# A hybrid decoder layer on one core: the order of the first transfers and the way through the last norm

## The chip, the cores and the metric

One Trainium2 chip, one of its cores. The metric is the time of one execution on the device in microseconds (us), the median of several runs; lower is better. One more execution was taken with the hardware profiler, and its trace is what the tables and rows below come from. The engines are TensorE (PE, and PEld for its weight loads), VectorE (DVE), ScalarE (ACT), GpSimd (POOL) and SyncE (SP), which issues the DMA transfers.

## The reference

One layer for 272 prompt tokens (16 learned ones and 256) and 8 decoding tokens together, 280 columns, with D_MODEL 2048 and D_FF 5504, all in float32. Cut to what matters here:

```python
def layer_norm(x, g, b):
    mu = jnp.mean(xf, axis=-1, keepdims=True)
    var = jnp.mean(jnp.square(xf - mu), axis=-1, keepdims=True)
    return ((xf - mu) * lax.rsqrt(var + LN_EPS)).astype(x.dtype) * g + b

def swiglu(x, w_gate, w_up, w_down):
    return (jax.nn.silu(x @ w_gate) * (x @ w_up)) @ w_down

def decoder_layer(x, ...):
    x = layer_norm(ALPHA * x + 0.5 * swiglu(x, f1_g, f1_u, f1_d), ln1_g, ln1_b)
    m, s_ret, s_hg = token_mixer(x, pos, s_ret, s_hg, prompt, w_in, lb, hg_norm_g, w_out)
    x = layer_norm(ALPHA * x + m, ln2_g, ln2_b)
    x = layer_norm(ALPHA * x + 0.5 * swiglu(x, f2_g, f2_u, f2_d), ln3_g, ln3_b)
    return x, s_ret, s_hg
```

The mixer projects to 10 times the width, runs two recurrent branches (retention with 8 heads, HGRN2 with 16), merges them by gates and projects back. The 16 learned tokens are dropped from the output, so behind the mixer there are 264 columns.

## The kernel before

Activations lie with features on the partitions and tokens along the free dimension: a tensor of width 2048 is 16 chunks (`KC`) of 128 features by 280 (or 264) columns. Weights are packed by the host into blocks of 128x128 in exactly the order in which they are used; eight blocks are a unit of 512 KB. `stream` hands them out: at the first block of a unit it issues the DMA into a tile `raw` (SyncE, L143), ScalarE rounds it to the short format `whi` (L145), VectorE takes the rest, `wlo` (L147). Each of the three tiles has three buffers, so unit u+3 waits for unit u. Activations are split in the same way into `xh` and `xl` (`split`, L176 and L177). `dense` then makes each product of two float32 blocks from three matmuls in the short format: high by high (L169), high weights by low activations (L170), low weights by high activations (L171), accumulated in PSUM.

The order of instructions on TensorE is that of the program. On the other engines a scheduler orders them by priority when the program is built, and `high_priority` puts the loading of a unit ahead of what stands earlier in the program. At the start this gives SyncE the order: three units, two chunks of tokens, three units, and so on; one DMA brings one chunk of tokens (L365).

`ffn` runs groups of two gate and two up blocks (four PSUM banks), 16 steps of k each; a group reads four blocks for each token chunk, so a unit covers two chunks. Then 16 down products, one chunk each, with 43 steps of k. `Norm` takes up each finished chunk: `chunk` adds alpha times the low and the high part of x to the product (L242, L243), `shifted` subtracts a common shift (the mean over chunk 0, found by `shift`), squares it on ScalarE and adds both to two running sums on VectorE. For the first two norms (`lead`) the chunk also goes on, scaled, to the next projection, whose matmuls begin before the statistics are known; `first` corrects their results, and `normalise` makes the normed chunks meanwhile. For the third norm `stats` sums over partitions by two products with a matrix of ones in full float32 (L285, L286; TensorE makes two matmul instructions of each such product), takes mean and variance, and `rsqrt` the reciprocal root with one Newton step, after a load of ScalarE's table for that function. Then `normalise` centres each chunk (VectorE), scales it by gain and root (VectorE, L320), adds the bias (ScalarE, L327) and stores it (SyncE, L328), 16 stores.

The scheduler also orders VectorE's and ScalarE's work in the mixer, where threads of small matmuls run between the dense ones.

Of the kernel before, what the change touches and what calls it, by code (L numbers as in the profile page):

```python
# [10 lines left out]
F32 = mybir.dt.float32  # L11
# [7 lines left out]
P = 128  # L19
# [12 lines left out]
U = 8  # L32


WP = P + 4
XP = 296
KSC = 1.0 / 16.0
LEVELS = (1, 2, 4, 8, 16, 32, 64)
MASKED = 5
# [58 lines left out]
def trunk(ctx: ExitStack, tc: tile.TileContext, A, O):  # L98
# [34 lines left out]
    nc.vector.memset(eps_h, EPS)  # L133


    def stream(w_dram):
        n_units = w_dram.shape[0]
        state = {"u": -1, "j": U, "hi": None, "lo": None}

        def load(u):  # L140
            with tc.high_priority():
                raw = wp.tile([P, U, P], F32, tag="raw", name=f"raw{u}", bufs=3)
                nc.sync.dma_start(raw, w_dram[u].rearrange("p (b c) -> p b c", b=U))  # L143
                hi = wp.tile([P, U, WP], F32R, tag="whi", name=f"whi{u}")[:, :, :P]
                nc.scalar.copy(hi, raw)  # L145
                lo = wp.tile([P, U, WP], F32R, tag="wlo", name=f"wlo{u}")[:, :, :P]
                nc.vector.tensor_tensor(out=lo, in0=raw, in1=hi.bitcast(F32), op=ALU.subtract)  # L147
# [12 lines left out]
        return block  # L160

    def dense(block, nk, outs, xhi, xlo, cols=slice(0, T), hook=None):
# [51 lines left out]
    def row_tile(name, n=T):  # L214
        return rp.tile([P, n], F32, tag=name, name=name)

    class Norm:
# [14 lines left out]
        def row(self, name):  # L232
            return row_tile(name)[:, : self.n]

        def chunk(self, m, f):
            n = self.n
            a = ALPHA if self.whole else 2.0 * ALPHA
            dx = row_tile(f"d{m}", T + 1)
            self.dx[m] = dx
            self.d[m] = d = dx[:, :n]  # L240
            x0 = xh[m].shape[1] - n
            nc.vector.scalar_tensor_tensor(out=d, in0=xl[m][:, x0:].bitcast(F32), scalar=a, in1=f, op0=ALU.mult, op1=ALU.add)  # L242
            nc.vector.scalar_tensor_tensor(out=d, in0=xh[m][:, x0:].bitcast(F32), scalar=a, in1=d, op0=ALU.mult, op1=ALU.add)  # L243
            if self.lead:
                nc.gpsimd.memset(dx[:, n : n + 1], 1.0)
            if self.c is None:
                self.waiting.append(m)
            else:
                self.shifted(m)

        def shift(self):
            n = self.n
            pc = mx_bank("pc")
            nc.tensor.matmul(pc[:, :n], ones, self.d[0], start=True, stop=True)
            self.c = self.row("lnc")
            nc.scalar.mul(self.c, pc[:, :n], 1.0 / P)
            self.s1, self.s2 = self.row("ls1"), self.row("ls2")
            for m in self.waiting:
                self.shifted(m)

        def shifted(self, m):
            n, d = self.n, self.d[m]
            sub(d, d, self.c)
            if m == 0:
                nc.scalar.copy(self.s1, d)
                nc.scalar.activation(self.s2, d, AF.Square)
            else:
                q = self.row("lnq")
                nc.scalar.activation(q, d, AF.Square)
                add(self.s1, self.s1, d)  # L270
                add(self.s2, self.s2, q)
            if self.lead:
                x_tiles(m, f"g{self.which}", n + 2)
                g = self.g[:, m : m + 1]
                dx = self.dx[m][:, : n + 1]
# [36 lines left out]
                ys.append(y)  # L312
            return ys

        def normalise(self, out=None):
            for c in range(KC):
                d = self.d[c]
                g, b = self.g[:, c : c + 1], self.b[:, c : c + 1]
                sub(d, d, self.mean)
                nc.vector.scalar_tensor_tensor(out=d, in0=d, scalar=g, in1=self.r, op0=ALU.mult, op1=ALU.mult)  # L320
                if out is None:
                    x_tiles(c, self.which, self.n)
                    nc.scalar.activation(xh[c], d, AF.Identity, bias=b)  # L323
                    nc.vector.scalar_tensor_tensor(  # L324
                        out=xl[c], in0=d, scalar=b, in1=xh[c].bitcast(F32), op0=ALU.add, op1=ALU.subtract)
                else:
                    nc.scalar.activation(d, d, AF.Identity, bias=b)  # L327
                    nc.sync.dma_start(out[c], d)  # L328

    def ffn(i, w_up, w_dn, which, before=None):  # L330

        n = T if before is None else TL
        cols = slice(0, n)
        with tc.tile_pool(name=f"h{i}", bufs=1) as hp:
            hh, hl = [None] * FC, [None] * FC
            block = stream(w_up)
            for gn, grp in enumerate(ffn_up_groups()):
                bank = acc_bank if gn % 2 == 0 else mx_bank
                outs = [bank(f"up{gn}_{j}") for j in range(len(grp))]
# [5 lines left out]
                for j in range(ng):  # L345
# [16 lines left out]
    with tc.tile_pool(name="inp", bufs=2) as ip:  # L362
        for c in range(KC):
            x0 = ip.tile([P, T], F32, tag=f"x0{c}", name=f"x0{c}", bufs=1)
            nc.sync.dma_start(x0, A["x"][:, c, :])  # L365
            x_tiles(c, 0)
            split(xh[c], xl[c], x0)
# [13 lines left out]
    nc.sync.dma_start(dec, A["dec"])  # L381
    nc.sync.dma_start(sel, A["sel"])

    norm1 = ffn(1, A["w_up1"], A["w_dn1"], 1)


    with tc.tile_pool(name="yp", bufs=1) as yp:
# [408 lines left out]
        norm2 = Norm(2, TL, True, True)  # L796
        for gn, grp in enumerate(out_groups()):
            outs = [acc_bank(f"wo{m}") for m in grp]
            dense(block, KC, outs, yh, yl, slice(0, TL), (lambda k: k == 6 and norm2.shift()) if gn == 1 else None)
            for m, o in zip(grp, outs):  # L800
                norm2.chunk(m, o[:, :TL])


    norm3 = ffn(2, A["w_up2"], A["w_dn2"], 3, norm2)
    norm3.stats()
    norm3.normalise(O["y"])


# [110 lines left out]
```

## Time and profile before

| | |
|---|---|
| median of 3 runs | 2869.44 us |
| the runs | 2877.39, 2869.44, 2869.11 us |
| the profiled execution | 2873.62 us |
| its span, first to last instruction | 2871.8 us |
| granted TensorE clock, mean | 0.994 |
| busy TensorE, VectorE, ScalarE | 2823.0, 1700.5, 1326.4 us |
| read from memory | 502.12 MB, 186 GB/s with what is written |

Busy time counts an engine's instructions, and a matmul's duration reaches over the beginning of the next, so a busy TensorE says only that matmuls follow each other. In rows of a timeline the first number is the start in us from the span's start, the second the time from the first to the last of the merged instructions; "xh<-x" names output and input tile, "x3" the count, and the bracket gives how long the engine was idle before and what ended that. Rows with "DMA" or "issue" ahead of a line come from the chain that ended last, followed back from the last instruction.

### The profile page before, as it was taken

The numbers are of one execution on the slowest core, as the hardware profiler recorded it, in microseconds if no ns is written. First come the engines' busy times: TensorE is split into PE (matmuls) and PEld (weight loads), VectorE is DVE, ScalarE is ACT, GpSimd is POOL, SyncE is SP. The second block draws the span as 40 slices with busy tenths as digits, with TensorE's granted clock in tenths as the row PEclk, the third lists the DMA queues.
The fourth block names the chain that finished last, engine by engine and source line by source line (L and its number), as shares of the span: only waits on it lengthen the run. The fifth ranks groups of instructions, "written<-read, shape, count | busy, mean of one in ns | idle before, by whom it ended". The sixth has DMA issues, their size and how long they took to land.

```text
span 2871.8 us, 54200 instructions
## 1 busy us (share of the span) xinstructions
PE 2823.0 (98%) x22642; PEld 2769.2 (96%) x22642; DVE 1700.5 (59%) x2690; ACT 1326.4 (46%) x1929; POOL 3.4 (0%) x38
## 2 busy tenths in 40 slices
PE   8999999999999999999999999999999999999997
PEld 8999999999999999899989898999999999999997
DVE  5444444455586766676757575766894444445555
ACT  4443334433353564545455554545454444444333
POOL 0000000000000000000000000000000000000000
PEclk9999999999999999999999999999999999999998
DMA  6555555555556665656665657564555555555553
GB/s 212 170 171 173 169 170 170 170 173 169 169 184 213 200 228 190 215 191 222 193 216 195 220 179 229 168 226 164 177 180 180 183 184 180 181 183 178 183 179 131
DMA packets 155717, 536.25 MB, mean 187 GB/s; under 512 B 18064, under 2 KB 27856, under 8 KB 155472
## 3 DMA queue, kind: packets, MB, share of 16 engines
q1 hardware_dynamic: 155472, 532.80, 57.5%
q8 instruction: 177, 2.90, 0.4%
q14 instruction: 68, 0.56, 0.1%
HBM read 502.12 MB, written 30.61 MB: 186 GB/s over the span
## 4 chain that ended last, share of the span: by engine, by line
PE 95%; ACT 1%; DMA 1%; DVE 1%; issue 0%; SPq 0%; ACTq 0%; DVEq 0%
PE up L170 12%; PE up L171 12%; PE up L169 12%; PE dn L169 6%; PE dn L170 6%; PE dn L171 6%; PE pj_g_r L169 1%; PE pj_v_r L169 1%; PE pj_k_r L169 1%; PE pj_f L169 1%; PE pj_g_h L169 1%; PE pj_v_r L170 1%; PE pj_k_r L170 1%; PE pj_f L170 1%; PE pj_f L171 1%; PE pj_k_r L171 1%
## 5 line engine op out<-in xcount | busy, mean ns | idle before, releaser
L147 DVE TENSOR_TENSOR wlo<-raw,whi 128x1024 fp32r<-128x1024 f32 x868 | 1062.7, 1224 | 916.6 <-ACT whi L145 911.5
L145 ACT CAST whi<-raw 128x1024 fp32r<-128x1024 f32 x868 | 909.4, 1048 | 1169.1 <-PE up L170 484.7
L169 PE MATMUL up<-xh,whi 128*128 128x280 f32 (+1 forms) x2688 | 772.9, 288 | 9.0 <-ACT xh L176 9.0
L170 PE MATMUL up<-xl,whi 128*128 128x280 f32 (+1 forms) x2688 | 774.3, 288 | 1.1 <-DVE xl L177 1.0
L171 PE MATMUL up<-xh,wlo 128*128 128x280 f32 (+1 forms) x2688 | 773.4, 288 | 0.0
L169 PEld LDWEIGHTS up<-xh,whi 128*128 128x128 f32 x2688 | 506.5, 188 | 9.2 <-ACT xh L176 9.2
L170 PEld LDWEIGHTS up<-xl,whi 128*128 128x128 f32 x2688 | 506.2, 188 | 1.8 <-DVE xl L177 1.8
L171 PEld LDWEIGHTS up<-xh,wlo 128*128 128x128 f32 x2688 | 506.6, 188 | 0.0
L169 PE MATMUL dn<-hh,whi 128*128 128x280 f32 (+1 forms) x1376 | 397.1, 289 | 0.0
L170 PE MATMUL dn<-hl,whi 128*128 128x280 f32 (+1 forms) x1376 | 395.8, 288 | 0.0
L171 PE MATMUL dn<-hh,wlo 128*128 128x280 f32 (+1 forms) x1376 | 395.8, 288 | 0.0
L170 PEld LDWEIGHTS dn<-hl,whi 128*128 128x128 f32 x1376 | 259.0, 188 | 0.1
L169 PEld LDWEIGHTS dn<-hh,whi 128*128 128x128 f32 x1376 | 258.9, 188 | 0.1
L171 PEld LDWEIGHTS dn<-hh,wlo 128*128 128x128 f32 x1376 | 258.6, 188 | 0.0
L169 PE MATMUL pj_g_r<-xh,whi 128*128 128x264 f32 x256 | 82.9, 324 | 0.0
L169 PE MATMUL pj_g_h<-xh,whi 128*128 128x264 f32 x256 | 77.3, 302 | 0.0
L170 PE MATMUL pj_i_h<-xl,whi 128*128 128x280 f32 x256 | 74.9, 293 | 2.4 <-DVE xl L324 2.4
L169 PE MATMUL pj_i_h<-xh,whi 128*128 128x280 f32 x256 | 75.0, 293 | 1.3 <-ACT xh L323 0.7
L169 PE MATMUL pj_v_r<-xh,whi 128*128 128x280 f32 x256 | 76.0, 297 | 0.0
L169 PE MATMUL pj_k_r<-xh,whi 128*128 128x280 f32 x256 | 75.9, 297 | 0.0
L170 PE MATMUL pj_v_r<-xl,whi 128*128 128x280 f32 x256 | 74.7, 292 | 0.0
L170 PE MATMUL pj_k_r<-xl,whi 128*128 128x280 f32 x256 | 74.6, 291 | 0.0
(310 smaller groups left out, 5154.2 us busy)
## 6 DMA issues: line engine op xcount, KB each, us to landing
raw<-in_w_up SPq DMA_DIRECT2D x344, 512.0 KB, 3.5
raw<-in_w_in SPq DMA_DIRECT2D x320, 512.0 KB, 3.5
raw<-in_w_dn SPq DMA_DIRECT2D x172, 512.0 KB, 3.5
smr<-in_sr SPq DMA_DIRECT2D x32, 512.0 KB, 5.6
out_srs<-smr SPq DMA_DIRECT2D x32, 512.0 KB, 4.3
raw<-in_w_out SPq DMA_DIRECT2D x32, 512.0 KB, 3.5
smh<-in_sg SPq DMA_DIRECT2D x16, 512.0 KB, 4.3
out_sgs<-smh SPq DMA_DIRECT2D x16, 512.0 KB, 6.1
```

The source lines that it names most:

```text
L145: nc.scalar.copy(hi, raw)
L147: nc.vector.tensor_tensor(out=lo, in0=raw, in1=hi.bitcast(F32), op=ALU.subtract)
L169: nc.tensor.matmul(o, wh, h, start=k == 0, stop=False)
L170: nc.tensor.matmul(o, wh, l, start=False, stop=False)
L171: nc.tensor.matmul(o, wl, h, start=False, stop=k == nk - 1)
```

## The change

At the start, the first unit is loaded in two parts of two and six blocks, the tokens in larger pieces, and the first transfers get fixed turns (0 first): chunk 0 on ScalarE's DMA queue, the unit's first part, its second, chunk 1, chunks 2 and 3, chunks 4 and 5. The other tokens (6 to 7, 8 to 11, 12 to 15) stand in the program's order. Seven products of the ones matrix with itself run on TensorE ahead of the first dense matmul; their results aren't used.

In the norms, the residual of a chunk (`residual`) is computed ahead of its dense product as soon as the shift is known (`ahead`), with the shift subtracted in it; behind the product one addition is left.

In the last norm `finish` takes the place of `stats` and `normalise`: the two sums over partitions take the running sums up to chunk 14, and chunk 15 and its square as second products of their own; the root is computed with the bias inside ScalarE's function, whose table an early activation loads behind the last gate block; five chunks are centred by VectorE, eleven by TensorE (identity by chunk plus identity by minus mean, in PSUM); VectorE multiplies by the root, ScalarE applies gain and bias, and two chunks go out in one store.

```diff
+WARM = 7
+PE_CENTRED = 11
...
+    def turn(n):
+        return tc.high_priority(offset=tc.tile_snap_priority() + 100 * (9 - n))
...
-        def load(u):
-            with tc.high_priority():
-                raw = wp.tile([P, U, P], F32, tag="raw", name=f"raw{u}", bufs=3)
...
+        def load(u, parts=((0, U, tc.high_priority),)):
...
+            for j0, j1, when in parts:
+                with when():
+                    nc.sync.dma_start(raw[:, j0:j1, :], src[:, j0:j1, :])
+                    nc.scalar.copy(hi[:, j0:j1, :], raw[:, j0:j1, :])
+                    nc.vector.tensor_tensor(out=lo[:, j0:j1, :], in0=raw[:, j0:j1, :], in1=hi[:, j0:j1, :].bitcast(F32), op=ALU.subtract)
...
+        if at_once:
+            state["hi"], state["lo"] = load(0, ((0, 2, lambda: turn(1)), (2, U, lambda: turn(2))))
+            state["u"] = state["j"] = 0
...
-        def chunk(self, m, f):
+        def residual(self, m, other, op):
...
-            nc.vector.scalar_tensor_tensor(out=d, in0=xl[m][:, x0:].bitcast(F32), scalar=a, in1=f, op0=ALU.mult, op1=ALU.add)
+            nc.vector.scalar_tensor_tensor(out=d, in0=xl[m][:, x0:].bitcast(F32), scalar=a, in1=other, op0=ALU.mult, op1=op)
             nc.vector.scalar_tensor_tensor(out=d, in0=xh[m][:, x0:].bitcast(F32), scalar=a, in1=d, op0=ALU.mult, op1=ALU.add)
...
+        def chunk(self, m, f):
+            if self.d[m] is not None:
+                add(self.d[m], self.d[m], f)
+                self.shifted(m)
+                return
+            self.residual(m, f, ALU.add)
...
+        def ahead(self, m):
+            if self.c is not None:
+                self.residual(m, self.c, ALU.subtract)
...
-                q = self.row("lnq")
+                self.q = q = self.row("lnq")
                 nc.scalar.activation(q, d, AF.Square)
+                if m == KC - 1 and not self.lead:
+                    return
...
+        def finish(self, out):
+            n = self.n
+            p1, p2 = mx_bank("p1"), mx_bank("p2")
+            for p, s in ((p1, self.s1), (p2, self.s2)):
+                nc.tensor.matmul(p[:, :n], ones, s, start=True, stop=False)
+            for p, s in ((p1, self.d[KC - 1]), (p2, self.q)):
+                nc.tensor.matmul(p[:, :n], ones, s, start=False, stop=True)
+            neg, v, r, t = self.row("lnc"), self.row("rv"), self.row("rr"), self.row("rt")
+            nc.scalar.activation(t, p1[:, :n], AF.Square, scale=1.0 / D)
+            nc.vector.scalar_tensor_tensor(out=v, in0=p2[:, :n], scalar=1.0 / D, in1=t, op0=ALU.mult, op1=ALU.subtract)
+            nc.scalar.mul(neg, p1[:, :n], -1.0 / D)
+            nc.scalar.activation(r, v, AF.Abs_reciprocal_sqrt, bias=eps_l)
...
+            centred = list(self.d)
+            for c in range(KC):
+                if c < KC - PE_CENTRED:
+                    add(self.d[c], self.d[c], neg)
                 else:
-                    nc.scalar.activation(d, d, AF.Identity, bias=b)
-                    nc.sync.dma_start(out[c], d)
+                    pd = (acc_bank if c % 2 else mx_bank)("pd")[:, :n]
+                    centred[c] = pd
+                    nc.tensor.matmul(pd, ident, self.d[c], start=True, stop=False)
+                    nc.tensor.matmul(pd, ident, neg, start=False, stop=True)
+            yo = ctx.enter_context(tc.tile_pool(name="yo", bufs=1))
+            for c0 in range(0, KC, 2):
+                y = yo.tile([P, 2, n], F32, tag=f"y{c0}", name=f"y{c0}")
+                for c in (c0, c0 + 1):
+                    mul(self.d[c], centred[c], r)
+                    nc.scalar.activation(
+                        y[:, c - c0, :], self.d[c], AF.Identity, scale=self.g[:, c : c + 1], bias=self.b[:, c : c + 1])
+                nc.sync.dma_start(out[c0 : c0 + 2].rearrange("c p t -> p c t"), y)
...
+            if before is not None:
+                warm = hp.tile([P, 1], F32, tag="warm", name="warm")
+                nc.scalar.activation(warm, sg[:, 0:1], AF.Abs_reciprocal_sqrt, scale=0.0, bias=eps_l)
             block = stream(w_dn)
             norm = Norm(which, n, False, i == 1)
             for m in range(KC):
                 o = acc_bank(f"dn{m}")
+                norm.ahead(m)
                 dense(block, FC, [o], hh, hl, cols, (lambda k: k == 6 and norm.shift()) if m == 1 else None)
                 norm.chunk(m, o[:, :n])
...
+        pw = mx_bank("pw")
+        for _ in range(WARM):
+            nc.tensor.matmul(pw[:, :P], ones, ones, start=True, stop=True)
+        up1 = stream(A["w_up1"], at_once=True)
+        for n, queue, c0, c1 in ((0, nc.scalar, 0, 1), (3, nc.sync, 1, 2), (4, nc.sync, 2, 4), (5, nc.sync, 4, 6)):
+            with turn(n):
+                tokens(queue, c0, c1)
+        for c0, c1 in ((6, 8), (8, 12), (12, KC)):
+            tokens(nc.sync, c0, c1)
...
-    norm3.stats()
-    norm3.normalise(O["y"])
+    norm3.finish(O["y"])
```

The norm behind the mixer calls `ahead` in the same way, and `tokens` issues one DMA for its chunks and splits each.

More of the change, by code (lines that the diff above doesn't have):

```diff
@@ L133, in trunk, with stream @@
     nc.vector.memset(eps_h, EPS)
[L136 removed]
+    def turn(n):
+        return tc.high_priority(offset=tc.tile_snap_priority() + 100 * (9 - n))
+    def stream(w_dram, at_once=False):
         n_units = w_dram.shape[0]
         state = {"u": -1, "j": U, "hi": None, "lo": None}
[L140 to L147 removed]
+        def load(u, parts=((0, U, tc.high_priority),)):
+            raw = wp.tile([P, U, P], F32, tag="raw", name=f"raw{u}", bufs=3)
+            hi = wp.tile([P, U, WP], F32R, tag="whi", name=f"whi{u}")[:, :, :P]
+            lo = wp.tile([P, U, WP], F32R, tag="wlo", name=f"wlo{u}")[:, :, :P]
+            src = w_dram[u].rearrange("p (b c) -> p b c", b=U)
+            for j0, j1, when in parts:
[3 more added lines that the diff above has]
+                    nc.vector.tensor_tensor(out=lo[:, j0:j1, :], in0=raw[:, j0:j1, :], in1=hi[:, j0:j1, :].bitcast(F32), op=ALU.subtract)
             return hi, lo
@@ L332, in ffn @@
+    def ffn(i, block, w_dn, which, before=None):
         n = T if before is None else TL
@@ L362, in trunk, with tokens @@
     with tc.tile_pool(name="inp", bufs=2) as ip:
[L363 to L367, printed above, removed]
+        def tokens(queue, c0, c1):
+            x0 = ip.tile([P, c1 - c0, T], F32, tag=f"x0{c0}", name=f"x0{c0}", bufs=1)
+            queue.dma_start(x0, A["x"][:, c0:c1, :])
+            for c in range(c0, c1):
+                x_tiles(c, 0)
+                split(xh[c], xl[c], x0[:, c - c0, :])
+        pw = mx_bank("pw")
[7 more added lines that the diff above has]
+            tokens(nc.sync, c0, c1)
         mf = ip.tile([P, MASKED + 1, 2 * P], F32, tag="mf", name="mf", bufs=1)
```

27 lines of the change are left out of this document (14 added, 13 removed).

## The prediction

> **What bounds the kernel now.** I read the page first, then the start and the end as timelines, then the chain of waits and some windows in between. The page:
>
> ```profile
> span 2871.8 us, 54200 instructions
> PE 95%; ACT 1%; DMA 1%; DVE 1%; issue 0%; SPq 0%; ACTq 0%; DVEq 0%
> ```
>
> The second line is the chain that ended last: 95% of the span is TensorE. Where TensorE streams, nothing that the change does to another engine can shorten the time; it can pay only where TensorE stands, and that is mostly ahead of the first matmuls and behind the last. Of the start, the timeline of SyncE's DMA issues, of ScalarE, of VectorE and of TensorE, and one row of the chain (start us, us, what, idle before in brackets):
>
> ```profile
> 0.73 1.33 SPq L143 DMA_DIRECT2D raw<-in_w_up  x3
> 2.11 1.06 SPq L365 DMA_DIRECT2D x<-in_x  x2
> 6.83 2.87 SPq L143 DMA_DIRECT2D raw<-in_w_up  x3
> 9.75 5.62 SPq L365 DMA_DIRECT2D x<-in_x  x10
> ...
> 4.50 1.04 ACT L145 CAST whi<-raw 128x1024 fp32r<-128x1024 f32 x1 [2.18 <-DMA raw<-in_w_up]
> 7.04 1.05 ACT L145 CAST whi<-raw 128x1024 fp32r<-128x1024 f32 x1 [0.25 <-DMA raw<-in_w_up]
> 8.00 0.74 ACT L176 CAST xh<-x 128x280 fp32r<-128x280 f32 x2
> 19.11 1.05 ACT L145 CAST whi<-raw 128x1024 fp32r<-128x1024 f32 x1 [0.65 <-PE up L170]
> 28.43 1.05 ACT L145 CAST whi<-raw 128x1024 fp32r<-128x1024 f32 x1 [2.05 <-PE up L170]
> ...
> 5.58 3.77 DVE L147 TENSOR_TENSOR wlo<-raw,whi 128x1024 fp32r<-128x1024 f32 x3 [4.57 <-ACT whi L145]
> ...
> 8.47 0.60 PE L169 MATMUL up<-xh,whi 128*128 128x280 f32 x1 [8.47 <-ACT xh L176]
> 12.50 0.43 PE L169 MATMUL up<-xh,whi 128*128 128x280 f32 x1
> 12.73 0.43 PE L170 MATMUL up<-xl,whi 128*128 128x280 f32 x1
> 13.26 0.29 PE L170 MATMUL up<-xl,whi 128*128 128x280 f32 x1
> 13.39 0.29 PE L171 MATMUL up<-xh,wlo 128*128 128x280 f32 x1
> ...
> 12.13 3.75 DMA x<-in_x
> ```
>
> Three units of weights (512 KB each) come ahead of the first tokens, so the first matmul waits until 8.47. Then three more weight issues, which wait for free buffers (6.83 to 9.70), stand in SyncE's queue ahead of token chunk 2, and the chain waits for it until 15.88. Up to 12.96 the matmuls follow each other in 0.23 us, afterwards in 0.13: half rate, then full. What all that costs: the cast at 19.11 waits for the matmuls of unit 1 and the one at 28.43 for those of unit 4, so 72 matmuls take 9.32 us, 0.129 each; 47 of them are done by 19.1, so a stream without a gap would have begun at 13.0.
>
> The end, as timelines of VectorE, TensorE, ScalarE and SyncE, and the DMA issues:
>
> ```profile
> 2851.51 0.43 DVE L242 SCALAR_TENSOR_TENSOR d<-xl,dn 128x264 f32<-128x264 f32 x1 [6.55 <-PE dn L171]
> 2853.39 0.71 PE L285 MATMUL p<-ls,ones 128*128 128x264 f32 x2 [1.92 <-DVE ls L188]
> 2853.94 0.68 PE L286 MATMUL p<-ls,ones 128*128 128x264 f32 x2
> 2854.14 0.39 ACT L288 ACTIVATE lnc<-p 128x264 f32<-128x264 f32 x1 [0.75 <-PE p L285]
> 2855.26 0.43 DVE L291 SCALAR_TENSOR_TENSOR lnq<-p,lnq 128x264 f32<-128x264 f32 x1
> 2856.26 1.28 ACT L199 ACT_TABLE_LOAD   x1
> 2857.55 0.42 ACT L199 ACTIVATE rr<-rv 128x264 f32<-128x264 f32 x1
> 2859.72 0.42 DVE L202 SCALAR_TENSOR_TENSOR rr<-rt,rr 128x264 f32<-128x264 f32 x1
> 2860.41 4.93 DVE L320 SCALAR_TENSOR_TENSOR d<-d,lnp,rr 128x264 f32<-128x264 f32 x12
> 2861.47 7.84 SPq L328 DMA_DIRECT2D out_y<-d  x16
> 2867.97 0.92 ACT L327 ACTIVATE d<-d,lnp 128x264 f32<-128x264 f32 x2 [0.57 <-DVE d L320]
> ...
> out_y<-d SPq DMA_DIRECT2D x16, 132.0 KB, 1.8
> ```
>
> The last dense product is read at 2851.51 and the span ends at 2871.8: 20.3 us in which TensorE does two products with the ones matrix. The reciprocal root is ready at 2860.14, VectorE scales 16 chunks at 0.41 each, and 2.9 us after ScalarE's last pass (2868.89) the last store has landed and the program has closed.
>
> **The start.** The change puts token chunk 0 first on ScalarE's DMA queue, and on SyncE's: two blocks of unit 0, its other six, chunk 1, chunks 2 and 3, chunks 4 and 5, and only then unit 1. Units 0 to 2 land 1.27 us apart (4.50 to 7.04 for two), 403 KB per us. Unit 0 landed at 4.50, so the first 268 KB (two blocks and chunk 0) by 3.9; 652 KB, all of unit 0, at 4.85; chunks 1 to 5 by 6.6 (1352 KB); unit 1 by 7.85 (1864 KB). Two casts of about 0.4 (chunk 0 is half of 0.74; a quarter of a unit lies between that and a quarter of 1.04) put the first matmul at 4.75 where it was 8.47. Its six matmuls and the other 18 of unit 0 wait for six blocks' cast and subtraction (three quarters of 1.04 and of 1.26, the mean of the three subtractions), so from 6.7 on they stream, and end near 8.8. Unit 1 is cast from 7.85 to 8.9 and subtracted by 10.15; its third matmul, the first that reads the low part, waits for that. The 21 matmuls that are then left of the 47 take 2.7, and unit 1's buffer is free at 13.1 where it was 19.1: 6.0 us. At the tokens' pace of the trace (ten of 140 KB in 5.62 us, 249 KB per us, waits included) 840 KB of tokens take 1.3 us longer, and 4.7 are left. With pairs in one transfer the 0.56 that one issue took there matters less, so I stay near the upper end: **5.6** (4.7 to 6.0).
>
> Seven products of the ones matrix run ahead of the first matmul. The trace has such products of 264 and 280 columns; 128 columns at 0.47 per 280 (rows below) are 0.21, and at half rate 0.43: 1.5 to 3.0 us from about 1.1, over by 4.1, and the loads are not there before 4.3, so they cost nothing. Half rate lasted from 8.47 to 12.96, 4.5 us from the first matmul; counted from the first ones product it ends near 5.6. If it doesn't, 24 matmuls of unit 0 at 0.23 last from 4.75 to 10.3, still about the time at which unit 1's low part is there: 0 to 0.5. ScalarE issues chunk 0's transfer (about 0.43 of its queue) when it has nothing else until 3.9. Under "DMA: Bandwidth & Descriptors", section "Anatomy of one DMA", the Trainium skill counts about 2.0 us fixed for each DMA beside bytes at 436 GB/s, and its rules ask for large transfers, which speaks against cutting unit 0 in two; the trace has three transfers landing 1.27 us apart, so the fixed part overlaps when issues follow each other. By that page alone the first 128 KB would be there 2.3 us after the issue at 0.73, at 3.0, and the sum would still hang on unit 1's subtraction.
>
> **The middle.** The residuals of a chunk are computed ahead of its dense product (two VectorE passes), with the shift subtracted in the first; afterwards one addition is left. Passes before: three; after: three. At the first two norms TensorE goes on with the next projection and reads chunk 15 last, so the shorter step there hides behind matmuls, as before: 0. The early activation `warm` moves a table load of 1.28 to the start of the second down projection, where ScalarE idles around 2 us between casts: 0, and it waits only for the last gate tile.
>
> **The end.** Before: two residual passes, the shift, a sum, then TensorE at 2853.39. After: one addition (2851.51 to 2851.95). The products of ones with the two running sums are queued right behind the last dense matmul, and those with chunk 15 and its square follow them. The price of one ones product of full precision:
>
> ```profile
> 817.32 0.64 PE L285 MATMUL p<-ls,ones 128*128 128x280 f32 x2
> 817.79 0.63 PE L286 MATMUL p<-ls,ones 128*128 128x280 f32 x2
> ```
>
> 0.47 to the next one at 280 columns, 0.443 at 264; in the end of the trace 0.55 (2853.39 to 2853.94). Four from 2851.47 end at 2853.25; the mean's are streamed by 2852.8 and readable 0.25 later (0.71 from start to end of such a product, 0.44 to 0.47 of it stream). ScalarE squares the mean and negates it (0.39 each, as `lnc`): minus mean at 2853.85. VectorE's variance, ScalarE's root without table load at 2854.45, three VectorE passes (2.2 before, from 2857.97 to 2860.14): root at 2856.65. From then 16 multiplications at 0.41 end at 2863.2, if their operands are there. Eleven chunks are centred by TensorE, two identity products each; the first of the 22 needs no mean, 21 wait for minus mean and nothing else is queued behind them: 21 times 0.443 is 9.3, from 2853.85 to 2863.15, readable at 2863.4. So TensorE sets the end, not VectorE: multiplication 0.43, ScalarE 0.5, at 2864.4. Then the 2.9 of before, and for the pair, 132 KB more at the stores' pace (16 in 7.84, 270 KB per us), 0 to 0.5: I take 0.3. End 2867.6, gain **4.2**. At 0.55 per product it is 2.0; with no additional store time 4.5. I take 0.443, from a stream at full clock, as the 22 are one. Eight issues in place of 16 take no queue time that counts.
>
> If the table had to be loaded again, the root would come 1.28 later and VectorE would end at 2864.5, 0.6 behind TensorE. The Trainium skill, "ScalarE: Activation LUTs", section "What ACT_TABLE_LOAD costs", gives 2.66 us with the drain; in this trace the activation follows the load of 1.28 after 0.01.
>
> **Sum.** 5.6 + 4.2 = 9.8 us. The profiled execution took 2873.62 us, 1.8 more than its span, so 2863.8 on its own basis; it lies 4.2 above the median of the runs, 2869.44. Subtracted from that: **2859.6**. What a measurement can tell here is 0.3%, 8.6 us.
>
> **Rivals.** Some rows on the clock and the mixer, windows (us, busy of PE, PEld, DVE, ACT, POOL, granted clock, DMA share, GB/s) and the chain:
>
> ```profile
> 1187.20:1190.60 3.40, 1.25 (x9) 1.13 (x10) 2.64 (x5) 3.37 (x5) 0.00 (x0) 1.00 1.01 395
> 1190.60:1194.00 3.40, 3.40 (x25) 1.90 (x24) 2.54 (x8) 1.50 (x3) 0.00 (x0) 0.50 0.60 201
> 2856.30:2871.80 15.50, 0.00 (x0) 0.00 (x0) 12.04 (x33) 8.47 (x18) 0.00 (x0) 0.50 0.41 140
> ...
> 1304.95 1.55 PE psc L709 x12
> 1450.85 1.55 PE psc L709 x12
> 1599.55 1.55 PE psc L709 x12
> ```
>
> *Half clock in the end.* A stretch of 3.4 us with TensorE busy for 1.25 was followed by one at clock 0.50, and the end is at 0.50 from 2856.3. If the centring products don't keep the clock, 5.5 of 21 are done by then and 15.5 take 0.89 each: 6.9 more, the end 2.7 later than before, 2.9 gained in all: 2866.5. Against it: TensorE would be busy nearly all the time from 2851.5. For it: no window of this trace holds such products alone. The Trainium skill, "TensorE: Matmul & The Clock Gate", section "HAM oscillation — how this bites in real kernels", asks for idle gaps above about 3.4 us; by that rule this case doesn't come; here a window only partly idle was enough. Chance 0.10.
>
> *Tokens behind weights again.* Chunks 6 and 7 may be queued behind units 3 to 5, as chunk 2 was; unit 5 waits for unit 2's subtraction (near 11.4 to 12.7), the tokens land 3.8 later and are split in 0.9, near 17.8, when they are due at 16.2: 1.6 lost, 2861.2. Chance 0.15.
>
> *Slower: more half-clock windows in the mixer.* From one head to the next it is 145.90 us (1304.95 to 1450.85), and 148.70 with such a window (1450.85 to 1599.55): 2.8 each. Where these windows fall depends on how the shorter start shifts the stages. Four more take the gain away (2871.0), seven, one for nearly every head, give 2879.2, slower by 0.34%. Against it: nothing in the mixer's order is changed. Chance 0.07; for the contrary, one such window fewer (2856.8), 0.06.
>
> *It doesn't do what it says:* the transfers come in the old order, only the end pays: 2865.2. Chance 0.04.
>
> **How the numbers follow.** The forecast has 0.58, its own range 2857.4 to 2861.5 (8 to 12 us gained). The range for 8 in 10, 2854.5 to 2867.0, takes in the half clock in the end and one window fewer, and leaves out the old order's and the mixer's bad cases at its edge. Faster by over 8.6: nine tenths of the forecast (0.52), 0.06 of the tokens' case, whose 8.2 is near the line, 0.06 of fewer windows: 0.64. Slower by over 8.6: most of the mixer's case, 0.06. The rest, 0.30, within.
>
> **What would show it.** Right: first dense matmul near 4.8, full rate from 6 to 9, unit 4's cast (the one that waits for unit 1) near 13; no load of a table behind the last dense matmul; products with the identity 0.44 to 0.45 apart at clock 1.00, the last of them some 12 us behind the last dense matmul; 16 us from the last dense product to the span's end. Wrong: those products 0.89 apart, a DMA of tokens releasing TensorE after 15 us, a table load in the end, heads in the mixer longer than 149 us.

## The result, and the profile after

The changed kernel takes **2859.37 us** (median of 7 runs, 2856.34 to 2863.62) against 2869.44 us (7 runs, 2865.44 to 2877.39): a ratio of 0.9962, interval 0.9949 to 0.9976, 10.1 us less. The forecast was 2859.6. The total was met, but not by the terms of the sum: the start gave 2.1 us of the forecast 5.6, the end 3.5 of 4.2, and the rest of the 10.1, about 4.5 us, stands in no row of the two ends and did not come again when both kernels were measured once more (e5_again). The two lines of the page after:

```profile
span 2857.5 us, 54281 instructions
PE 94%; DMA 2%; ACT 2%; DVE 1%; issue 1%; SPq 0%; ACTq 0%; DVEq 0%
```

TensorE is still 94% of the chain; DMA and ScalarE have 2% each where they had 1%. The start, as timelines of SyncE's issues, of ScalarE and of TensorE, and below the last gap two pieces of the chain of waits (start us, us, what). In all timelines "..." marks rows left out:

```profile
1.65 1.37 SPq L430 DMA_DIRECT2D x<-in_x  x3
3.06 3.86 SPq L156 DMA_DIRECT2D raw<-in_w_up  x3
6.96 0.43 SPq L430 DMA_DIRECT2D x<-in_x  x1
10.86 4.19 SPq L156 DMA_DIRECT2D raw<-in_w_up  x3
15.11 0.42 SPq L430 DMA_DIRECT2D x<-in_x  x1
...
16.99 1.05 ACT L157 CAST whi<-raw 128x1024 fp32r<-128x1024 f32 x1 [0.59 <-PE up L184]
22.15 1.08 ACT L190 CAST xh<-x 128x280 fp32r<-128x280 f32 x3 [4.10 <-DMA x<-in_x]
...
1.05 3.36 PE L438 MATMUL pw<-ones 128*128 128x128 f32 x14 [1.05 <-DVE eps_h L137]
4.59 0.40 PE L183 MATMUL up<-xh,whi 128*128 128x280 f32 x1 [0.19 <-ACT whi L157]
10.89 0.39 PE L185 MATMUL up<-xh,wlo 128*128 128x280 f32 x1 [0.73 <-DVE wlo L158]
22.62 0.39 PE L183 MATMUL up<-xh,whi 128*128 128x280 f32 x1 [2.42 <-ACT xh L190]
...
6.59 5.69 DMA raw<-in_w_up
15.11 7.02 DMA x<-in_x
```

The first dense matmul is at 4.59 instead of 8.47 and runs at full rate almost at once; unit 1's low part comes at 10.89. But then three weight issues, units 4 to 6, take SyncE from 10.86 to 15.05, because each waits until VectorE has done with a buffer. Unit 6 waits longest, for unit 3, whose transfer lands only at 12.28 and whose subtraction ends at 14.70. VectorE and SyncE, in a window that takes the merged rows apart:

```profile
13.47 1.23 DVE L158 TENSOR_TENSOR wlo<-raw,whi 128x1024 fp32r<-128x1024 f32 x1 [1.39 <-ACT whi L157]
14.72 0.33 SPq L156 DMA_DIRECT2D raw<-in_w_up  x1
```

Chunks 8 to 11 are issued behind it at 15.11, land at 22.13, and TensorE stands for 2.4 us until 22.62. So the first up-projection issues its last matmul at 542.37 instead of 544.51.

The end, as timelines of VectorE, TensorE, ScalarE and SyncE:

```profile
2840.75 0.43 DVE L202 TENSOR_TENSOR d<-d,dn 128x264 f32<-128x264 f32 x1 [6.55 <-PE dn L185]
2845.07 0.43 DVE L372 SCALAR_TENSOR_TENSOR rr<-rt,rr 128x264 f32<-128x264 f32 x1
2852.46 0.43 DVE L199 TENSOR_TENSOR d<-pd,rr 128x264 f32<-128x264 f32 x1 [0.46 <-PE pd L381]
...
2851.37 0.61 PE L380 MATMUL pd<-d,ident 128*128 128x264 f32 x2
2851.82 0.61 PE L381 MATMUL pd<-lnc,ident 128*128 128x264 f32 x2
...
2843.07 0.52 ACT L368 ACTIVATE rr<-rv,eps_l 128x264 f32<-128x264 f32 x1 [0.31 <-DVE rv L366]
2846.22 8.08 ACT L387 ACTIVATE y<-d,lnp 128x264 f32<-128x264 f32 x16 [2.64 <-DVE d L199]
...
2847.35 7.35 SPq L389 DMA_DIRECT2D out_y<-y  x8
```

The last dense product is read at 2840.75, the span ends at 2857.5: 16.8 us instead of 20.3. The root comes without a table load, the identity products are 0.445 apart and done by 2852.43. ScalarE's 16 passes are one block without a pause from 2846.22 to 2854.30, (8.08 − 0.59)/15 = 0.50 apart: they set the end, and the products and multiplications run ahead of them.

### The profile page after: what moved, and what is told of

It is laid out like the page before. It is cut to its first block, busy times and chain, and to the rows that moved or that the text cites. A ratio compares the mean times of both kernels' runs of the same rounds, so it can differ in the third digit from the quotient of the medians.

```text
span 2857.5 us, 54281 instructions
## 1 busy us (share of the span) xinstructions
PE 2829.5 (99%) x22704; PEld 2775.9 (97%) x22704; DVE 1688.2 (59%) x2677; ACT 1328.4 (46%) x1931; POOL 3.4 (0%) x38
## 4 chain that ended last, share of the span: by engine, by line
PE 94%; DMA 2%; ACT 2%; DVE 1%; issue 1%; SPq 0%; ACTq 0%; DVEq 0%
PE up L184 12%; PE up L185 12%; PE up L183 12%; PE dn L183 6%; PE dn L184 6%; PE dn L185 6%; PE pj_v_r L183 1%; DMA smr<-in_sr 1%; PE pj_g_r L183 1%; PE pj_k_r L183 1%; PE pj_v_r L184 1%; PE pj_k_r L184 1%; PE pj_k_r L185 1%; PE pj_v_r L185 1%; PE wo L183 1%; PE pj_f L183 1%
## 5 line engine op out<-in xcount | busy, mean ns | idle before, releaser
L158 DVE TENSOR_TENSOR wlo<-raw,whi 128x1024 fp32r<-128x1024 f32 (+1 forms) x869 | 1063.5, 1224 | 916.7 <-ACT whi L157 912.5
L157 ACT CAST whi<-raw 128x1024 fp32r<-128x1024 f32 (+1 forms) x869 | 909.7, 1047 | 1159.8 <-PE up L184 484.2
```

Of the source, the lines that this page charges most:

```text
L157: nc.scalar.copy(hi[:, j0:j1, :], raw[:, j0:j1, :])
L158: nc.vector.tensor_tensor(out=lo[:, j0:j1, :], in0=raw[:, j0:j1, :], in1=hi[:, j0:j1, :].bitcast(F32), op=ALU.subtract)
```

## The experiments

Three stretches are compared in all traces: when the last matmul of the first up-projection is issued (the start's sum), how long the tail is (from the issue of the last dense matmul to the span's end), and the mixer from its first to its last `psc` product; beside it stand TensorE's waits for the small product `pst` in the mixer, which e5 explains. The stretches between (first down-projection, output projection, second feed-forward block) last the same in every trace within 0.05 us; those right ahead of the mixer's first `psc` product (96.4 to 100.1 us) and behind its last (103.0 to 106.7) vary from trace to trace.

| kernel | median us (runs) | ratio to the kernel before | first up ends | mixer | waits of `pst` | tail |
|---|---|---|---|---|---|---|
| before | – | 1 | 544.51 | 992.18 | 11.8 | 20.57 |
| changed | 2859.37 (7) | 0.9962 [0.9949, 0.9976] | 542.37 | 983.07 | 9.5 | 17.11 |
| e1_start | 2868.50 (11) | 0.9998 [0.9989, 1.0007] | 543.86 | 986.32 | 13.4 | 20.57 |
| e2_tail | 2864.37 (11) | 0.9986 [0.9977, 0.9995] | 545.18 | 983.80 | 10.2 | 18.02 |
| e3_ahead | 2867.92 (11) | 1.0002 [0.9993, 1.0011] | 544.08 | 986.85 | 11.8 | 19.63 |
| e4_turns | 2860.14 (11) | 0.9979 [0.9970, 0.9988] | 538.81 | 981.63 | 7.3 | 17.12 |
| e5_again | 2860.27 (12) | 0.9980 [0.9972, 0.9989] | 542.20 | 978.37 | 6.7 | 17.11 |
| e6_gain | 2863.3 (1) | – | 541.62 | 986.59 | 11.1 | 16.31 |
| e7_centre | 2862.68 (1) | – | 541.53 | 981.24 | 10.4 | 20.89 |
| e8_cold | 2863.82 (1) | – | 540.03 | 990.55 | 10.9 | 17.11 |
| e9_later | 2850.38 (5) | 0.9942 [0.9929, 0.9955] | 544.56 | 973.47 | 0 | 17.11 |
| e10_best | 2848.87 (5) | 0.9934 [0.9922, 0.9946] | 541.68 | 973.50 | 0 | 16.31 |

e1 to e4 stand beside a kernel before of 2868.25 us (33 runs), e5, e6, e9 and e10 beside one of 2866.11 us (17 runs), e7 and e8 beside one run of 2868.6. Medians are therefore compared through their own kernel before.

**e1_start: the start alone.** The kernel before with the transfers' turns and the ones products, the norms as they were:

```diff
-        for c in range(KC):
-            x0 = ip.tile([P, T], F32, tag=f"x0{c}", name=f"x0{c}", bufs=1)
-            nc.sync.dma_start(x0, A["x"][:, c, :])
...
+        up1 = stream(A["w_up1"], at_once=True)
+        for n, queue, c0, c1 in ((0, nc.scalar, 0, 1), (3, nc.sync, 1, 2), (4, nc.sync, 2, 4), (5, nc.sync, 4, 6)):
...
-    norm1 = ffn(1, stream(A["w_up1"]), A["w_dn1"], 1)
+    norm1 = ffn(1, up1, A["w_dn1"], 1)
```

> The start alone (ones products, order and parts of the first transfers); norms and end as before. Theory A (each end saves what its own rows show, and the middle, from the end of the first up projection to the last dense matmul, changes only by chance): the first up projection ends 2.1 us earlier than before's 544.5, the end takes 20.3 us from the last dense matmul as before, the time falls by about 2 us plus or minus the spread of the middle. Theory B (the shorter start shifts the mixer against the windows of the clock, and that saves over 4 us in the mixer): the time falls by 6 us or more, and the mixer takes about 982 us from the first to the last score product where it took 991. Theory C (the early residuals shorten the middle): 2 us, mixer near 991.

Measured: 2868.50, no change that can be measured (0.9989 to 1.0007, so at most 3.2 us gained). In its trace the first stage ends only 0.65 us earlier than before. The wait for chunks 8 to 11 is there again (1.8 us), and two windows show a second price (us, busy of PE, PEld, DVE, ACT, POOL, granted clock, DMA share, GB/s):

```profile
20.80:24.20 3.40, 1.50 (x10) 1.26 (x10) 1.17 (x3) 2.04 (x5) 0.00 (x0) 1.00 1.00 383
24.20:27.60 3.40, 3.40 (x17) 3.40 (x16) 2.31 (x4) 1.07 (x3) 0.00 (x0) 0.51 0.93 339
```

The window with the wait, busy for 1.50 of 3.40, is followed by one at clock 0.51, with 17 matmuls where 28 fit at full rate: 11 times 0.129, 1.4 us. The Trainium skill, "TensorE: Matmul & The Clock Gate", section "HAM oscillation — how this bites in real kernels", ties this to idle gaps above about 3.4 us; here a gap of 1.8 was enough, as the prediction had read from the mixer's rows. Theory B is out, since the time did not fall by 6 us; the mixer's 986.32 us lie between the 982 and the 991 of the theories and decide nothing.

**e2_tail: the end alone, without the early residuals.** The kernel before with `finish`, the table's early load and the paired stores, but with the residual computed behind the product; of its edits, the call:

```diff
-    norm3.stats()
-    norm3.normalise(O["y"])
+    norm3.finish(O["y"])
```

> The end alone: sums with chunk 15 as products of their own, centring by TensorE, early table, paired stores; the start as before, no early residuals. Theory A: from the last dense matmul to the span's end about 17.7 us (the two residual passes and the shift of chunk 15 are back on the path, 0.9 us more than the changed kernel's 16.8); the time falls by about 2.6 us. Theories B and C: the same, the mixer near 991 us.

Measured: 2864.37, 3.9 us less (1.4 to 6.6), and the tail is 18.02, 2.55 shorter. The 17.7 expected was worked out from 16.8, which counts from the read of the last dense product, 0.3 us behind its issue; from the issue it is 18.0.

**e3_ahead: the early residuals alone.** The kernel before with `residual` and `ahead`, the old `stats` and `normalise`:

```diff
+                norm.ahead(m)
...
+            norm2.ahead(grp[0])
```

> The early residuals alone, in all three norms; start and end as before. Theory A: 0.9 us saved behind the last dense matmul, nothing else: 0 to 1 us faster. Theory C (the early residuals shorten the middle): 4 to 9 us faster, the mixer near 982 us. Theory B: as A.

Measured: 2867.92, unchanged (2.0 us less to 3.2 more); the tail is 19.63, 0.94 shorter, which is two VectorE passes. 2.55 and 0.94 make 3.49, and the changed kernel's tail is 3.46 shorter: the two parts of the end add up. The first two norms gave nothing that shows, as forecast.

**e4_turns: no tokens behind weights.** The changed kernel with turns for units 1 and 2 and for all remaining tokens, so that no token chunk is issued behind a unit that waits for a buffer:

```diff
...
-        for c0, c1 in ((6, 8), (8, 12), (12, KC)):
-            tokens(nc.sync, c0, c1)
+        up1.early(1, 6)
+        up1.early(2, 7)
+        for n, c0, c1 in ((8, 6, 8), (9, 8, 12), (10, 12, KC)):
+            with turn(n):
+                tokens(nc.sync, c0, c1)
```

> The changed kernel with the other tokens in turns as well: units 1 and 2 get fixed turns behind chunks 4 and 5, then chunks 6 and 7, 8 to 11, 12 to 15, then unit 3. Theory: in the changed kernel tokens 8 to 11 stood behind unit 5 in the queue, and TensorE waited 2.7 us for them near 22 us and 0.5 more for their low part: all of it goes, the first up projection ends near 539.2 (542.4 in the changed kernel, 544.5 before), and the time is 3.2 us under the changed kernel's. Rival: the bytes bind, not the order, and the wait moves to units 3 and 4, which now come behind all tokens: less than 1 us.

TensorE's waits in the first 60 us (waited for: us in total, times, longest us), of the changed kernel and of this one:

```profile
PE up L183 <- ACT xh L190: 2.4, 1, 2.4
PE up L185 <- DVE wlo L158: 1.2, 2, 0.7
PE pw L438 <- DVE eps_h L137: 1.0, 1, 1.0
PE up L183 <- ACT whi L157: 0.9, 2, 0.7
```

```profile
PE up L187 <- DVE wlo L159: 1.2, 2, 0.7
PE pw L440 <- DVE eps_h L137: 1.0, 1, 1.0
PE up L185 <- ACT whi L158: 0.3, 1, 0.3
```

The wait for `xh` is gone, and the first stage ends at 538.81: 3.56 earlier than in the changed kernel and 5.70 earlier than before. That is the size of the forecast term of 5.6, in one profile with no tokens queued behind units that wait; e10 has the same turns, and there the stage ends 2.83 earlier than before. In the median it can't be told from the changed kernel (8.1 us less than its kernel before, beside 5.8 in e5; the intervals overlap).

**e5_again: the changed kernel, unchanged, once more.** Start and end give 2.14 + 3.46 = 5.6 us by the traces, the first measurement gave 10.1.

> The changed kernel once more, unmodified, beside before on the same chip. Theory A (the ends save 2.1 and 3.5 us by their rows, the mixer's length is chance): 5.6 us under before's median, ratio 0.9980; the 10.1 of the first seven runs held 4.5 us of luck in the middle. Theory B (the middle is shorter for a reason, the shifted start or the early residuals): again 9 to 10 us, ratio 0.9966.

Measured: 2860.27 against 2866.11, 5.8 us (3.2 to 8.0). That fits the 5.6, and so do e1 to e3, whose medians add up to 4.0; by this about 4.5 of the first result were chance, an estimate, since the intervals of the two measurements (6.9 to 14.6 and 3.2 to 8.0) just overlap. Most of it lay on the side of the kernel before: its median went from 2869.44 to 2866.11, the changed kernel's from 2859.37 to 2860.27. How such a difference arises is seen in the first profiled pair: of the 14.3 us between the two spans 9.1 lie in the mixer (992.18 and 983.07), whose instructions stand in the same order on every engine. What moves there are waits of the small product `pst` for ScalarE's copy `ktm`. TensorE's waits from 800 to 2010 us, of before, changed and e5_again:

```profile
PE pst L645 <- ACT ktm L629: 11.8, 8, 2.5
```

```profile
PE pst L722 <- ACT ktm L706: 9.5, 8, 1.8
```

```profile
PE pst L722 <- ACT ktm L706: 6.7, 8, 1.8
```

The same kernel has 9.5 and 6.7 us of it. Behind some of these waits comes a window at half clock: four stretches of them in before's mixer, one in the changed kernel's, none in e5's profile.

**e6_gain: the gain on VectorE.** The changed kernel with ScalarE's pass reduced to the bias:

```diff
-                    mul(self.d[c], centred[c], r)
-                    nc.scalar.activation(
-                        y[:, c - c0, :], self.d[c], AF.Identity, scale=self.g[:, c : c + 1], bias=self.b[:, c : c + 1])
+                    nc.vector.scalar_tensor_tensor(
+                        out=self.d[c], in0=centred[c], scalar=self.g[:, c : c + 1], in1=r, op0=ALU.mult, op1=ALU.mult)
+                    nc.scalar.activation(y[:, c - c0, :], self.d[c], AF.Identity, bias=self.b[:, c : c + 1])
```

> The changed kernel with the gain multiplied in by VectorE's pass (one instruction with two operands, 0.41 each before) and only the bias on ScalarE. Theory (ScalarE's 16 passes with gain and bias follow each other in 0.505 us and set the end, not TensorE's centring): passes 0.41 apart as before's, ScalarE waits for the last centred chunks, the end takes 16.2 us from the last dense matmul where it took 17.1. Rival (TensorE or VectorE sets the pace): 17.1 or more.

ScalarE's timeline in its tail:

```profile
2850.98 6.33 ACT L388 ACTIVATE y<-d,lnp 128x264 f32<-128x264 f32 x15 [2.70 <-DVE d L386]
2857.69 0.51 ACT L388 ACTIVATE y<-d,lnp 128x264 f32<-128x264 f32 x1 [0.38 <-DVE d L386]
```

The passes now follow VectorE, which follows the identity products; the last one waits for VectorE. The tail is 16.31: 4.26 shorter than before, where 4.2 was forecast with TensorE at the end of the chain. One run gives no verdict on the median (the mixer of its profile was 3.5 us longer than the changed kernel's), the tail does.

**e7_centre: no centring by TensorE.** The changed kernel with VectorE adding minus mean to all 16 chunks:

```diff
-PE_CENTRED = 11
+PE_CENTRED = 0
```

> The changed kernel with VectorE centring all 16 chunks of the last norm and no identity products. Theory A (ScalarE's 16 passes follow the first VectorE product, so what stands ahead of that product moves the whole end): 11 more additions at 0.34 us stand before the first product, 3.7 us, and the end of the kernel, 17.11 us from the last dense matmul's issue to the span's end, becomes 20.8 (20.3 to 21.3), longer than in the kernel before (20.57). Rival B (ScalarE's own 8.1 us of passes hide VectorE's additions): the end stays within 0.5 us of 17.1.

VectorE and ScalarE in its tail:

```profile
2844.94 4.21 DVE L202 TENSOR_TENSOR d<-d,lnc 128x264 f32<-128x264 f32 x12
2849.06 5.59 DVE L199 TENSOR_TENSOR d<-d,rr 128x264 f32<-128x264 f32 x16
2849.53 8.08 ACT L387 ACTIVATE y<-d,lnp 128x264 f32<-128x264 f32 x16 [6.42 <-DVE d L199]
```

Eleven more additions stand ahead of the first multiplication, and ScalarE's same 8.08 begins that much later: the tail is 20.89, 3.78 longer, as the first theory had it (20.8). It is longer than the kernel before's 20.57, so without TensorE's centring, and with all additions ahead of the multiplications, the new end would gain nothing.

**e8_cold: no ones products.** The changed kernel with `WARM = 0`:

```diff
-WARM = 7
+WARM = 0
...
-        pw = mx_bank("pw")
```

> The changed kernel without the seven ones products at the start. Theory A (the first dense matmuls at half rate only eat into waits for unit 0's and unit 1's later parts, which TensorE meets anyway before 11 us): the first dense matmul stays at 4.4 to 4.8 us, the first ones run 0.26 us apart instead of 0.13, and the first stage ends within 1 us of the 542.2 to 542.4 that the two profiles of the changed kernel have. Rival B (every half-rate window is paid): a window of 3.4 us or two more at half rate, and the first stage ends 1.7 to 3.4 us later, at 544 to 545.7.

TensorE's timeline:

```profile
4.32 0.60 PE L183 MATMUL up<-xh,whi 128*128 128x280 f32 x1 [4.32 <-ACT whi L157]
8.80 0.44 PE L185 MATMUL up<-xh,wlo 128*128 128x280 f32 x1
9.03 0.37 PE L183 MATMUL up<-xh,whi 128*128 128x280 f32 x1
11.02 0.40 PE L185 MATMUL up<-xh,wlo 128*128 128x280 f32 x1 [0.73 <-DVE wlo L158]
```

The matmuls are 0.23 apart up to 9.03, yet unit 1's low part is still waited for, and comes at 11.02. In the profiles of the same start with the ones products it comes at 10.89 to 11.69, so half rate cost nothing that can be told from their spread. Nor do the ones products bring full rate for certain: e1 has them, and its matmuls are 0.23 apart from 5.30 to 10.52, the case for which the prediction allowed 0 to 0.5 us. The first stage even ended at 540.03, outside the first theory's 1 us and the other way from the rival: the tokens 8 to 11 landed in time in this run and the wait at 20 us was absent. With one run it stays open whether leaving the ones products out helps that, or whether the transfers just fell well.

**e9_later: `pst` later.** The changed kernel with another wait taken away, the mixer's: the thread that makes `ktm` lets ten steps of dense work pass before `pst`, and six behind it:

```diff
                     nc.sync.dma_start(O["sgs"][2 * u + h], sm)
-                    yield 6
+                    yield 10
...
                     nc.sync.dma_start(O["sgp"][2 * u + h], S[:, 2, :])
-                    yield 10
+                    yield 6
```

> The changed kernel, with the three products for a head's HGRN2 state put four steps of the dense work later and what follows them four steps nearer, so that ScalarE has some 3 us more for the copies they read. Theory (the mixer's spread comes from those waits, up to 2.5 us each, 9.5 to 12 us in all, and from the 3.4 us windows at half clock that follow some of them): the wait for the copy falls under 2 us in all, the heads take 143 to 145 us each where they took 145.8 to 150, 8 to 14 us faster than the changed kernel, and no half-clock window in the mixer. Rival (ScalarE's queue binds there, the wait comes back at the next products): under 3 us.

Measured: 2850.38, 15.7 us less than its kernel before (0.9929 to 0.9955), and 9.9 less than the changed kernel in e5. Its waits from 800 to 2010 us have no line for `pst` any more; the first is now

```profile
PE pd L196 <- ACT prodsmh L190: 3.9, 2, 2.0
```

and the mixer lasts 973.47, 4.9 us less than in e5's profile and 9.6 less than in the changed kernel's first. From the second head on, each takes 144.96 to 145.05 us, where the changed kernel's took 145.83 to 148.42. One expectation failed: a window at clock 0.50 is still there, at 968.93, in the first head. The start of this profile shows how far chance goes there too: a wait of 3.0 for the tokens, half clock behind it, and the first stage ends at 544.56, no earlier than in the kernel before.

**e10_best: all three.** The changed kernel with the edits of e4, e6 and e9.

> All that the rows point to together: units 1 and 2 and all tokens in turns (first up projection at 538.8), the state's products four steps later, and in the last norm the gain multiplied in by VectorE with the root, ScalarE adding the bias alone. Theory: 3.5 us from the tokens, 0.9 in the end and 8 to 14 in the mixer under the changed kernel's time: 2848 us, 2844 to 2852. Rival (the mixer's wait only moves): 2857.

Measured: **2848.87** (2846.90 to 2849.09), 0.9934 of the kernel before, the lowest median here: 17.2 us less. Tail 16.31 and mixer 973.50 repeat e6 and e9. The start ends at 541.68, not at e4's 538.81: a wait of 1.5 us for unit 1's high part and a window at clock 0.50 from 12.4 took 2.9 back. In its chain of waits TensorE's identity products end the kernel, as forecast for the change itself:

```profile
2841.50 0.45 PE pd L382 x2
2841.95 0.46 PE pd L383 x2
2842.43 0.50 DVE d L388
2842.96 0.52 ACT y L390
```

## Why the prediction was right in its total, and where its steps failed

**The start, 5.6 forecast, 2.1 measured.** The step to unit 1 held: first matmul 4.59 for 4.75, full rate near 5.3 for 5.6, unit 1's low part 10.89 for 10.15, the 47th matmul at 13.56 where it was at 18.78. 5.2 us were gained there. The failed step is the equation with "a stream without a gap": what unit 1 gained was taken for what the stage gains, but a gap followed. From 19.91 to 22.62 TensorE issues nothing, 2.6 us more than one pitch, and the next two matmuls follow after 0.49 and 0.23 instead of 0.13: together 3.0, and 2.2 are left. This is the rival "tokens behind weights again", chance 0.15, with the right mechanism (a unit's issue waits for a buffer and the tokens queue behind it), one transfer and one unit later than it said (chunks 8 to 11 behind unit 6, not 6 and 7 behind unit 5) and at nearly twice its price of 1.6, as the landing took 7.0 us where 3.8 was reckoned. It should have been the likely case: the row of 10.86 follows from the same three buffers as the row 6.83 of before. e4's profile shows the term whole, 5.70, when its cause is taken away; e10's, with the same cause taken away, shows 2.83.

The 2.1 is itself one draw. In the other profiles with this start and the ones products the stage ends 2.3 (e5), 2.9 (e6), 3.0 (e7) and 0.65 (e1) earlier than before, and in e9 no earlier. In e6 the wait for the tokens is absent, but unit 1's high part comes 1.5 us late and a window at clock 0.50 follows. None reaches the forecast range of 4.7 to 6.0: the sum took every landing from one pace of transfers, and their landings vary.

The fixed 2.0 us that the prediction takes from the Trainium skill, "DMA: Bandwidth & Descriptors", section "Anatomy of one DMA", stand there for transfers that GpSimd issues. Here ScalarE issued chunk 0 (140 KB) at 0.73, and its cast begins at 3.81, 3.1 us later, where an estimate from that section would be 2.3.

**The end, 4.2 forecast, 3.46 measured.** All that TensorE does came as worked out: products 0.445 apart at full clock, the last streamed at 2852.43 where the sum, moved to this trace (10.76 us earlier by the read of the last dense product), has 2852.39; root at 2845.5 for 2845.89, no table load; stores 3.23 behind the last pass for 3.2. The failed step is "So TensorE sets the end, not VectorE … ScalarE 0.5": ScalarE's 16 passes were priced as one pass behind the last multiplication. In the kernel before they had only a bias and kept up with 0.41; the change gives them the gain as well. Every pass is longer, by the groups of the two kernels (duration ns min/median/max):

```profile
L327 ACT ACTIVATE d<-d,lnp x16: 498/499/516, 2860.9 to 2868.4; 128x264 f32<-128x264 f32 x16
```

```profile
L387 ACT ACTIVATE y<-d,lnp x16: 590/591/607, 2846.2 to 2853.7; 128x264 f32<-128x264 f32 x16
```

At 0.50 apart 16 of them take 8.1 us, more than the identity products leave them. The forecast gain moved into this new bound: 0.66 us at the last pass, 0.8 in the tail by e6, where taking the gain off ScalarE brings 4.26. The Trainium skill has the price, in "ScalarE: Activation LUTs", section "What ACT_TABLE_LOAD costs": 93 ns for each operand that is a pointer to one value per partition, and as much overlap between passes; the traces agree (499 and 591). The prediction drew on that section for the table alone.

**The middle, 0 forecast.** By the traces of e1 to e3 that holds: the early residuals gain only in the last norm. But the stretch is not still: its length varied by 13.8 us from profile to profile (978.37 to 992.18 among the ten whose mixer has the same code). The rival "more half-clock windows" priced only the windows; the waits for `ktm`, 6.7 to 13.4 us, some of them just ahead of such windows, were missing from the prediction's reading though they stand in before's waits with 11.8. That they lengthen the mixer is shown by e9 and e10, where they are gone and it takes 973.5 us both times; between the other profiles its length doesn't follow them alone (13.4 us of waits with 986.32, 11.8 with 992.18), as the half-clock windows differ too. Why the waits differ from run to run is not shown. ScalarE's work ahead of `ktm` follows the landing of states from memory, which may make transfers the source, but no run separates that.

**The total.** 5.6 us of true terms, taken from the median of 2869.44, would have been 2863.8: inside the range, 4.5 from the first result. That the forecast of 9.8 and the first result of 10.1 agree is chance, terms 4.2 too large beside runs of the kernel before that came out long; the repetition gave 5.8.

**The signs.** Table load in the end: none. Products 0.89 apart: no. Last identity product 12 us behind the last dense matmul: 12.0. Heads of the mixer over 149 us: none in the changed kernel's trace, the longest took 148.42. Unit 4's cast near 13: no, it waited for its transfer until 15.35. "A DMA of tokens releasing TensorE after 15 us" was named as what would prove the forecast wrong, and the chain shows exactly this piece at 15.11. So the start's step was wrong by the prediction's own sign, though the total agreed.

## What to carry to other kernels

When an engine's instruction gets one more job (here the gain in ScalarE's pass), price the whole row of such instructions as a possible bound, not the one at the end of the chain. When transfers are put in a set order, follow the queue past the last one that was given a place: the next issue that waits for a buffer holds up all behind it. And a total that agrees proves no term: measure each by itself, and repeat the first result before it is explained.

## What the runs showed of the hardware

**When a wait costs a second time.** In e1, e9 and e10 a wait of 1.8, 3.0 and 1.5 us was followed by 3.41 us at clock 0.50, which costs about 1.4 us more; the changed kernel's own wait of 2.4 us was not. The difference lies in where the wait falls. In every trace that has several stretches at clock 0.50 they begin whole multiples of 3.413 us apart (in before's at 1190.62, 1484.16 and 1634.35: 86 and 44 times), so each trace can be cut into windows on that grid. e9's wait, from about 20.6 to 23.60, lies almost wholly in one window:

```profile
20.03:23.44 3.41, 0.59 (x5) 0.36 (x3) 0.00 (x0) 0.32 (x1) 0.00 (x0) 1.00 0.95 376
23.44:26.85 3.41, 3.25 (x13) 3.06 (x14) 2.84 (x6) 2.79 (x7) 0.00 (x0) 0.50 0.81 332
```

The changed kernel's, on the grid of its own stretches (1772.72 and 2854.74), is shared by two:

```profile
18.27:21.68 3.41, 1.93 (x15) 1.70 (x14) 1.03 (x1) 0.00 (x0) 0.00 (x0) 1.00 0.96 269
21.68:25.09 3.41, 2.38 (x16) 2.17 (x17) 2.05 (x4) 2.59 (x6) 0.00 (x0) 1.00 1.02 410
25.09:28.50 3.41, 3.41 (x28) 3.41 (x27) 2.58 (x6) 2.22 (x5) 0.00 (x0) 1.00 0.78 303
```

Counted so over all twelve traces, from 8 us to the last dense matmul and for windows at full clock: TensorE busy for less than 1.6 us was followed by clock 0.50 in 20 of 20 windows, busy for 1.6 to 2.1 us in 14 of 42, and busy for more in none of over 9800. What decides between 1.6 and 2.1 these runs don't show, nor what sets the grid against the kernel's start, which differs from profile to profile.
